# Layer 0's first modulation sums on four TensorE column strips, and a pooling mixer with channels on partitions

## The chip, the core and the metric

The kernel runs on one core of one Trainium2 chip. The metric is device time in microseconds (us) of one execution, as the median of several. Five engines of the core appear below: PE (TensorE, matrix products; PEld is its weight load), DVE (VectorE), ACT (ScalarE), POOL (GpSimd) and SP (SyncE, whose queue issues every DMA of this kernel).

## The reference, cut to what matters

A trunk of two layers over 256 tokens of 2048 channels, all in float32. Layer 0 mixes tokens by pooling, layer 1 by latent attention; each mixer is followed by a SwiGLU feed-forward network (FFN) of 5632 hidden units. What the change concerns is layer 0 up to its FFN:

```python
sc = jax.nn.silu(c)                                   # [1, 2048]
shift_m, scale_m, gate_m, shift_f, scale_f, gate_f = jnp.split(sc @ mod_w[0] + mod_b[0], 6, axis=-1)
h = modulate(rmsnorm(x, norm_mix[0]), shift_m, scale_m)      # h*(1+scale)+shift
# pool_mixer: in each of 4 groups of 512 channels, the mean over the last 2, 4, 8 or 16 tokens less h,
# times a 512x512 matrix of the group, times pool_scale
y = pool_mixer(h, pool_w[0], pool_scale[0])
x = x + gate_m[:, None, :] * y
h = modulate(rmsnorm(x, norm_ffn[0]), shift_f, scale_f)
x = x + gate_f[:, None, :] * swiglu(h, ffn_gate[0], ffn_up[0], ffn_down[0])
```

The six vectors of 2048 are sums over 2048 rows of `mod_w[0]`, 16.8 MB of weights each.

## The kernel before, in words

Tokens are two tiles of 128, channels 16 row tiles of 128 (`KD`) or 4 chunks of 512 (`ND`, `CH`). All weights pass through one pool of six load buffers (`raw`, 1 MB each). Their DMAs are issued in program order by SP, and a load waits until its buffer has been read by the work that used it six loads earlier. PSUM is eight banks (`ps`). Each engine executes its own instructions strictly in a fixed order that a scheduler (or, between `tc.manual_schedule()` lines, the text) set when the program was built.

**The front**, up to the first product of the FFN, does this:

1. Small loads, `x`, the statistics of `x` (`stat_piece`, L410: ACT squares and sums a 128x512 piece; eight pieces; then `rstd`).
2. Shift of the mixer, then scale (`mod_part`, class `Part`): for each of 16 row tiles a 1 MB load, and one DVE instruction (L183) that multiplies the 128x2048 tile by a column of silu(c) and adds it to an accumulator. At the end 16 PE products with ones (L275, `to_cols`) sum over partitions and put the vector on partitions. Between the two sums PE makes the pooled means of `x` (L719 to L728, four groups).
3. The gate (`SharedPart`): 11 row tiles on DVE, five (`GM_PE`) on PE as products with a replicated column (L200), so that the gate stands on all partitions in four banks.
4. Mixer: modulated means (L797, L799), times the group's matrix (L784, 64 instructions with tokens on the output's partitions), copied by ACT (L786), scaled by `pool_scale` on DVE (L791), times the gate, added to `x` and squared again (`add_gated`, L525, L526, L410). This stretch is in an order written out by hand, in which units of the next sums (`pump`) are placed among the steps.
5. Shift and scale of the FFN's first 512 channels (`BlockPart` with `shared`): eight units of two row tiles of 2x512 columns, 1 MB; half of the tiles on PE (L230, one output row), half on DVE (L233); the ends are summed by 16 small products (L247). The result goes to `cols` (L737, L738).
6. The first chunk of the normed stream is scaled (L432), turned (L444), modulated (L458, L459) and meets the first FFN weights, which ACT and DVE split into two parts (L368, L370): the first product of L392.

After that the FFN and layer 1 run as one long row of PE products (L392), with the remaining modulation sums ("background") loaded and added on DVE beside them; this part of the source is the same in both kernels.

## Time and profile before

| | |
|---|---|
| runs, us | 1964.61, 1965.02, 1966.27 (median 1965.02) |
| profiled execution: span from first to last instruction, us | 1962.3 |
| busy in the span, us | PE 1853.0, PEld 1520.7, DVE 1546.4, ACT 850.0, POOL 35.9 |
| loaded and stored | 572.66 MB, mean 292 GB/s |
| mean granted TensorE clock | 0.983 |

The profile is of one execution. A row of the timeline gives the start in us, the time from there to the end of the last of its instructions, the engine, the source line, the operation with its output and inputs, the count, and in brackets how long the engine had stood idle and what ended that. In a table of stretches each engine has its busy time and (x) its instructions, then come the granted PE clock (PEclk), the share of time in which the DMA engines were busy, and the rate. SPq rows are issues of DMAs, not their duration. A row that lists minimum, median and maximum gives the duration of single instructions in ns. A float32 product is two PE instructions ("passes").

### The profile page before, as it was taken

Reading aid. Unit: us, or ns where it says so; the run is one execution under the profiler, and the core shown is the slowest. Engines: PE = TensorE matmul, PEld = TensorE weight load, DVE = VectorE, ACT = ScalarE, POOL = GpSimd, SP = SyncE. Lnnn points to the kernel's source line nnn. Section 1 sums busy time; section 2 is a strip of 40 time slices with the busy share of each in tenths; the row PEclk is TensorE's granted clock in tenths of the full one; section 3 lists DMA queues with packets and bytes.
Section 4 is the critical chain, followed back from the end, with each engine's and each line's share of the span. In section 5 each row is a group of like instructions: output and inputs, shape, how many; then the busy total and the mean of one; then the engine's idle time right before and its main releaser. Section 6 shows DMA issues by size and latency. Waiting matters only on the chain. (4 is left out here: it accounts for less than half of the span.)

```text
span 1962.3 us, 21516 instructions
## 1 busy us (share of the span) xinstructions
PE 1853.0 (94%) x8485; PEld 1520.7 (77%) x8485; DVE 1546.4 (79%) x1312; ACT 850.0 (43%) x939; POOL 35.9 (2%) x33
## 2 busy tenths in 40 slices
PE   0489999999999999998999999999999999999998
PEld 0444888888888888886789987888888888888886
DVE  7887899998778778888989975889986566554556
ACT  3123544444443333334676744544444433343333
POOL 1000000000000000000000000000000000000000
PEclk9889999999999999999899999999999999999999
DMA  9999998898898989987888684989887667665561
GB/s 377 408 378 365 379 321 305 310 350 327 313 329 302 332 325 345 338 333 284 307 311 304 228 295 142 360 303 325 297 293 260 225 229 257 235 209 186 195 219 70
DMA packets 225184, 572.66 MB, mean 292 GB/s; under 512 B 11958, under 2 KB 16286, under 8 KB 203442
## 3 DMA queue, kind: packets, MB, share of 16 engines
q1 hardware_dynamic: 225084, 571.30, 80.9%
q8 instruction: 66, 1.08, 0.2%
q14 instruction: 34, 0.28, 0.0%
HBM read 564.97 MB, written 6.29 MB: 291 GB/s over the span
## 5 line engine op out<-in xcount | busy, mean ns | idle before, releaser
L392 PE MATMUL ps<-hl,act 128*128 128x512 f32 x7008 | 1609.5, 391 | 4.7 <-ACT act L459 2.2
L392 PEld LDWEIGHTS ps<-hl,act 128*128 128x128 f32 x7008 | 1315.1, 188 | 279.3 <-ACT act L459 4.4
L370 DVE TENSOR_TENSOR hl<-raw,hl 128x2048 fp32r<-128x2048 f32 x296 | 676.2, 2289 | 239.9 <-ACT hl L368 236.1
L368 ACT ACTIVATE hl<-raw 128x2048 fp32r<-128x2048 f32 x296 | 566.4, 1919 | 608.7 <-PE ps L392 542.1
L183 DVE SCALAR_TENSOR_TENSOR acc<-raw,s_col,acc 128x2048 f32<-128x2048 f32 x155 | 364.0, 2348 | 4.2 <-DMA raw<-in_mod_w_dram 1.6
L233 DVE SCALAR_TENSOR_TENSOR acc<-raw,s_col,acc 128x1024 f32<-128x1024 f32 x121 | 155.0, 1281 | 8.7 <-DMA raw<-in_mod_w_dram 7.2
L556 DVE TENSOR_TENSOR act<-ps,act 128x512 f32<-128x512 f32 x96 | 64.6, 687 | 14.1 <-PE ps L392 13.7
L275 PE MATMUL ps<-ones,acc 128*128 128x1 f32 x64 | 13.9, 352 | 62.8 <-DVE acc L183 39.9
L410 ACT ACTIVATE junk<-x 128x512 bf16<-128x512 f32 x40 | 25.2, 630 | 89.6 <-DVE x L526 44.1
L275 PEld LDWEIGHTS ps<-ones,acc 128*128 128x128 f32 x64 | 13.8, 332 | 64.5 <-DVE acc L183 41.4
L590 ACT ACTIVATE act<-ps 128x512 fp32r<-128x512 f32 x44 | 23.8, 596 | 61.5 <-PE ps L587 53.4
L625 DVE TENSOR_TENSOR x<-ps,x 128x512 f32<-128x512 f32 x32 | 22.1, 691 | 35.4 <-PE ps L392 35.4
L458 ACT ACTIVATE t2k<-ps,cols 128x256 f32<-128x256 f32 x64 | 33.2, 567 | 21.6 <-PE ps L444 17.0
L634 ACT ACTIVATE t2k<-ps 128x512 f32<-128x512 f32 x24 | 14.2, 593 | 64.2 <-PE ps L392 64.2
L918 PE MATMUL ps<-act,hl 128*128 128x256 f32 x128 | 37.2, 291 | 0.6 <-DVE hl L370 0.6
L919 PE MATMUL ps<-act,hl 128*128 128x256 f32 x128 | 36.7, 287 | 0.0
L920 PE MATMUL ps<-act,hl 128*128 128x256 f32 x128 | 36.1, 286 | 0.0
L591 DVE TENSOR_TENSOR act<-ps,act 128x512 fp32r<-128x512 f32 x44 | 28.2, 685 | 8.1 <-ACT act L590 8.0
L638 DVE TENSOR_TENSOR t2k<-ps,t2k 128x512 f32<-128x512 f32 x24 | 16.6, 690 | 21.3 <-PE ps L392 21.3
L444 PE MATMUL ps<-con,t2k 128*128 128x128 f32 x144 | 22.5, 306 | 11.2 <-DVE t2k L432 8.1
L784 PE MATMUL ps<-act,act 128*128 128x512 f32 x64 | 30.7, 644 | 0.9 <-issue 0.9
L554 ACT ACTIVATE act<-ps 128x512 f32<-128x512 f32 x32 | 19.1, 598 | 28.3 <-PE ps L392 28.1
(168 smaller groups left out, 955.0 us busy)
## 6 DMA issues: line engine op xcount, KB each, us to landing
raw<-in_mod_w_dram SPq DMA_DIRECT2D x128, 1024.0 KB
raw<-in_ffn_gate_dram SPq DMA_DIRECT2D x88, 1024.0 KB
raw<-in_ffn_up_dram SPq DMA_DIRECT2D x88, 1024.0 KB
raw<-in_ffn_down_dram SPq DMA_DIRECT2D x88, 1024.0 KB
raw<-in_mod_w_dram SPq DMA_DIRECT2D x128, 512.0 KB
raw<-in_kv_mod_w_dram SPq DMA_DIRECT2D x32, 1024.0 KB
raw<-in_w_o_dram SPq DMA_DIRECT2D x16, 1024.0 KB
raw<-in_w_uq_dram SPq DMA_DIRECT2D x8, 768.0 KB
```

The costliest lines, as they stand in the source:

```text
L183: dve.scalar_tensor_tensor(out=self.acc, in0=r, scalar=s_col[:, self.kt:self.kt + 1], in1=self.acc, op0=ALU.mult, op1=ALU.add)
L233: dve.scalar_tensor_tensor(out=self.acc, in0=r[:, k], scalar=s_, in1=self.acc, op0=ALU.mult, op1=ALU.add)
L368: hi_ins = act.activation(hi, r, AF.Copy)
L370: lo_ins = dve.tensor_tensor(out=lo, in0=r, in1=hi.bitcast(F32), op=ALU.subtract)
L392: pe.matmul(banks[tok], lhsT=t_[:, i, k, tok * P:(tok + 1) * P], rhs=w[:, k, :], start=first and n < len(part), stop=last and n >= len(ord ...
L458: act.activation(full, pts[k // 2][:, k % 2, :], AF.Identity, scale=scale, bias=bias)
L556: dve.tensor_tensor(out=part, in0=banks[tok], in1=part, op=ALU.add)
L591: dve.tensor_tensor(out=m[:, 1, :, ts_], in0=v, in1=m[:, 0, :, ts_].bitcast(F32), op=ALU.subtract)
L784: pe.matmul(pt, lhsT=pooled[g // 2][:, g % 2, k, tok * P:(tok + 1) * P], rhs=wp[g][:, k, :], start=k == 0, stop=k == KL - 1)
L918: pe.matmul(pt[:, h, :], lhsT=wl(h0 + h, k), rhs=t_[:, 0, k, :], start=k == 0, stop=False)
L919: pe.matmul(pt[:, h, :], lhsT=wh(h0 + h, k), rhs=t_[:, 0, k, :], start=False, stop=False)
L920: pe.matmul(pt[:, h, :], lhsT=wh(h0 + h, k), rhs=t_[:, 1, k, :], start=False, stop=k == KL - 1)
```

## The change

- **Column strips.** Shift, scale and gate of the mixer and the first block of the FFN's shift and scale are summed on PE alone. A new tile `front` holds silu(c) in column 0 of 32-column blocks, zeros elsewhere; its part `s_strip[:, kt, :]` is the stationary operand (128x32). A 1 MB weight tile is multiplied by four products (`StripPart`), each on 512 of its columns and each writing 32 of the 128 partitions of one PSUM bank; in `StripBlock` the four are two row tiles by shift and scale. After the last tile `strip_columns` copies the bank with ACT and turns it with four products by a selector (`sel`, `pair`: new constants), which gives the vector on partitions. DVE adds the bias, which is loaded and turned once (`brows`, `bcol`).
- **Mixer with channels on partitions.** `x` is turned as it comes (`xT`, eight banks of four transposes). The group products have the channels on the output's partitions (L835, 128x256), and `pool_scale` is folded into the gate column (`gm_col`). DVE adds gate times product to `xT` (L849); PE turns the result back (L855), ACT copies token tile 0 of it and DVE token tile 1 into `x`, and the statistics follow.
- **Order of loads.** The small loads come first, then four tiles of the shift, then `x` and the band matrices. `tc.manual_schedule()` around the mixer is gone.
- `SharedPart`, `GM_PE`, the shared form of `BlockPart`, `psc` and the loads for it are removed.

```diff
+    class StripPart:
+        def unit(self):
+            if self.kt == 0:
+                self.bank = ps_t()
+            r = raw_t([P, D])
+            sync.dma_start(r, self.w[self.kt * P:(self.kt + 1) * P, :])
+            for i in range(NSTRIP):
+                pe.matmul(self.bank[i * STRIP:(i + 1) * STRIP, :], lhsT=s_strip[:, self.kt, :],
+                          rhs=r[:, i * CH:(i + 1) * CH], start=self.kt == 0, stop=self.kt == KD - 1)
+            self.kt += 1
+            if self.kt == KD:
+                self.done(strip_columns(self.bank, sel))
...
+    def strip_columns(bank, picks):
+        rows = t2k([P, CH])
+        act.activation(rows, bank, AF.Copy)
+        n = picks.shape[1]
+        pt = ps_t()
+        for b in range(KL):
+            pe.matmul(pt[:, b * n:(b + 1) * n], lhsT=rows[:, b * P:(b + 1) * P], rhs=picks, start=True, stop=True)
...
-    push(mod_part(0, 0, shift_to(C_SM0, to_cols)))
-    push(mod_part(0, 1, scale_to(C_AM0, V_NM, to_cols)))
-    pump(KD)
+    push(strip_cols(0))
+    push(strip_cols(1, vcol[:, V_NM:V_NM + KD]))
+    pump(4)
+    for tok in range(NT):
+        load_x(tok)
...
+    pump(KD - 4)
...
+    xT = [act_t([P, 2, KL, T], F32) for _ in range(2)]
+    for g in range(ND):
+        for h2, pt in enumerate(turned_pieces([x[:, tok, g * CH:(g + 1) * CH] for tok in range(NT)])):
+            act.activation(xT[g // 2][:, g % 2, 2 * h2:2 * h2 + 2, :], pt, AF.Copy)
...
-    gm = SharedPart(a["mod_w"][0][:, cs], a["mod_b"][0:1, cs], lambda acc: None)
-    push(gm)
-    for j in range(ND):
-        push(sf_block(0, j, C_SF0, C_AF0, j == 0), KD // 2)
+    push(strip_cols(2, ps_col))
+    push(first_block(), KD // 2)
+    for j in range(1, ND):
+        push(sf_block(0, j, C_SF0, C_AF0), KD // 2)
...
+                pe.matmul(pt[:, i, :], lhsT=wp[g][:, k, ns], rhs=pooled_of(g * KL + k), start=k == 0,
+                              stop=k == KL - 1)
...
+            with urgent():
+                dve.scalar_tensor_tensor(out=stream_of(kt), in0=pooled_of(kt), scalar=gm_col[:, kt:kt + 1],
+                                         in1=stream_of(kt), op0=ALU.mult, op1=ALU.add)
+        for tok in range(NT):
+            with urgent():
+                pt = ps_t()
+                for k in range(KL):
+                    pe.transpose(pt[:, k * P:(k + 1) * P], stream_of(g * KL + k)[:, tok * P:(tok + 1) * P], ident)
+                piece = x[:, tok, g * CH:(g + 1) * CH]
+                if tok == 0:
+                    act.activation(piece, pt, AF.Copy)
+                else:
+                    dve.tensor_copy(piece, pt)
+                stat_piece(tok, g)
```

**Where instructions stand, first place: the pooled means.** Before, PE's queue has these rows at the end of the shift (`acc_163`) and at the first group of means (`hl_120` is the band, `t2k` pieces of the normed `x`); the sums themselves are on DVE.

```order
L275 MATMUL ps_214<-ones,acc_163 128x1 x16
L719 MATMUL ps_239<-hl_120,ones 128x256
L720 MATMUL ps_239<-hl_120,ones 128x128
L726 MATMUL ps_243<-hl_120,t2k_235 128x256
L727 MATMUL ps_243<-hl_120,t2k_237 128x128
```

Now PE's queue has, at the same place, the last tile of the shift (`raw_250`), the selection (L216), the turning of `x` (two of eight banks shown), the first and the last rows of the four groups of means, and behind them the first tile of the scale (`raw_398`).

```order
L230 MATMUL ps_105<-raw_250,front 32x512 x4
L216 MATMUL ps_258<-con,t2k_256 128x4 x4
L465 MATMUL ps_269<-con,x 128x128 x4
L465 MATMUL ps_310<-con,x 128x128 x4
L750 MATMUL ps_321<-hl_132,ones 128x256
L757 MATMUL ps_391<-hl_132,t2k_377 128x256
L758 MATMUL ps_391<-hl_132,t2k_379 128x128
L230 MATMUL ps_397<-raw_398,front 32x512 x4
```

What moved: the sums of the scale now stand in the same queue as the pooled means, behind all of them.

On SP the loads around that place now read as follows (`raw_250` is the last load of the shift, `raw_398` to `raw_428` the first six of the scale, `raw_434` the seventh, which takes the buffer of `raw_398`).

```order
L228 DMA raw_250<-in_mod_w_dram 128x2048
L228 DMA raw_398<-in_mod_w_dram 128x2048
L228 DMA raw_428<-in_mod_w_dram 128x2048
L809 DMA act_503<-in_pool_w_dram 128x4x512
L228 DMA raw_434<-in_mod_w_dram 128x2048
```

One load of the group matrices stands ahead of `raw_434`, the other three behind the scale's last load.

**Second place: the end of the front.** Before, PE's queue ends the front with the last of L230, the turning of the first chunk of the normed stream (L444), the end of the first block (L247), and the first product of the FFN.

```order
L230 MATMUL ps_589<-raw_676,s_col 1x512
L444 MATMUL ps_682<-con,t2k_666 128x128
L247 MATMUL ps_695<-ones,t2k_696 128x1 x4
L247 MATMUL ps_695<-ones,acc_585 128x1 x8
L392 MATMUL ps_749<-hl_722,act_726 128x512
```

Now it ends with the block's last unit (L251), one of its four selections, the turning back of the stream (L855, 32 rows, the first and the last shown), the other selections, the turning of the first chunk, and the first product.

```order
L251 MATMUL ps_745<-raw_795,front 32x512 x4
L216 MATMUL ps_804<-con,t2k_802 128x2
L855 MATMUL ps_823<-con,act_267 128x128
L855 MATMUL ps_843<-con,act_267 128x128
L216 MATMUL ps_804<-con,t2k_802 128x2 x3
L855 MATMUL ps_891<-con,act_268 128x128 x4
L465 MATMUL ps_909<-con,t2k_905 128x128
L413 MATMUL ps_941<-hl_814,act_919 128x512
```

And ACT's queue behind the gate has the copy of the block's bank, the split of the first FFN weights, four copies into `x`, eight squares with a second split among them, and the modulation (L479).

```order
L212 ACTIVATE t2k_802<-ps_745 128x512
L389 ACTIVATE hl_814<-raw_812 128x2048
L858 ACTIVATE x<-ps_823 128x512
L858 ACTIVATE x<-ps_843 128x512
L431 ACTIVATE junk_829,ssq_818<-x 128x512
L431 ACTIVATE junk_877,ssq_818<-x 128x512
L389 ACTIVATE hl_979<-raw_977 128x2048
L431 ACTIVATE junk_897,ssq_818<-x 128x512
L479 ACTIVATE t2k_920<-ps_909,cols 128x256
```

What moved: the stream's turning back, its copies and its statistics stand behind the block's last unit; before, the stream's statistics (L410 after L526) stood beside the block's sums on other engines, and only L444 to L459 were behind them.

More of the change, by code (lines that the diff above doesn't have):

```diff
@@ L47 @@
 C_FOLD = C_SIGN + 1
-C_END = C_FOLD + P
+C_SEL = C_FOLD + P
+C_PAIR = C_SEL + 4
+C_END = C_PAIR + 2
 BAND_W = T + P
@@ L184, in add @@
                                      in1=self.acc, op0=ALU.mult, op1=ALU.add)
-    class SharedPart(Part):
-        def add(self, r):
-            if self.kt == 0:
-                self.banks = [ps_t() for _ in range(ND)]
-            if self.kt not in GM_PE:
-                super().add(r)
-                return
-            rep = t2k([P, P])
-            act.activation(rep, ones, AF.Copy, scale=s_col[:, self.kt:self.kt + 1])
-            for j in range(ND):
-                js = slice(j * CH, (j + 1) * CH)
-                if self.kt == KD - 1:
-                    pe.matmul(self.banks[j], lhsT=ones, rhs=self.acc[:, js], start=False, stop=False)
-                pe.matmul(self.banks[j], lhsT=rep, rhs=r[:, js], start=self.kt == GM_PE[0], stop=self.kt == KD - 1)
+    def strip_columns(bank, picks):
[5 more added lines that the diff above has]
+            pe.matmul(pt[:, b * n:(b + 1) * n], lhsT=rows[:, b * P:(b + 1) * P], rhs=picks, start=True, stop=True)
+        return pt[:, :KL * n].rearrange("p (b i) -> p i b", i=n)
@@ new lines, in tile_trunk, with __init__, unit @@
+    class StripBlock:
+        def __init__(self, w, col, done):
+            self.w, self.col, self.done, self.kt = w, col, done, 0
+        def unit(self):
+            if self.kt == 0:
+                self.bank = ps_t()
+            r = raw_t([P, 2, 2, CH])
+            rows = self.w[self.kt * P:(self.kt + 2) * P, :].rearrange("(k p) (i n) -> p k i n", p=P, i=2)
+            for k in range(2):
+                sync.dma_start(r[:, k], rows[:, k, :, self.col:self.col + CH])
+            for k in range(2):
+                for i in range(2):
+                    m = (2 * k + i) * STRIP
+                    pe.matmul(self.bank[m:m + STRIP, :], lhsT=s_strip[:, self.kt + k, :], rhs=r[:, k, i, :],
+                              start=self.kt == 0, stop=self.kt == KD - 2)
+            self.kt += 2
+            if self.kt == KD:
+                self.done(strip_columns(self.bank, pair))
@@ L821, in tile_trunk @@
+    rstd = stat_finish()
+    first = modulated(turned_pieces(scaled(rstd, 0, True)), 0, C_AF0, C_SF0)
     push(mod_part(0, 5, gate_to("ffn0")))
```

180 lines of the change are left out of this document (80 added, 100 removed).

## The prediction

> **What bounds the kernel now.** I read the page first: the slices of the span and the chain that ended last.
>
> ```profile
> PE   0489999999999999998999999999999999999998
> PEclk9889999999999999999899999999999999999999
> DMA  9999998898898989987888684989887667665561
> ...
> PE 38%; ACT 0%; DVE 0%; issue 0%; POOLq 0%; ACTq 0%
> ```
>
> A slice is 49 us. PE is full from the fourth on, and as far back as the chain reaches it is PE. The change touches only what comes before, the first 184 us, where PE is idle or half busy and the DMA engines are full. So I asked for stretches: the start, a quiet piece, the three around a dip, the block's loads, and the FFN.
>
> ```profile
> 0.00:4.00 4.00, 0.00 (x0) 0.00 (x0) 0.00 (x0) 1.59 (x2) 3.47 (x8) 1.00 0.51 164
> 20.00:40.00 20.00, 0.00 (x0) 0.00 (x0) 18.87 (x9) 3.59 (x7) 0.00 (x0) 1.00 1.02 422
> 143.00:146.00 3.00, 3.00 (x9) 1.33 (x8) 3.00 (x3) 0.00 (x0) 0.00 (x0) 1.00 0.06 25
> 146.00:149.00 3.00, 3.00 (x9) 1.33 (x8) 0.42 (x1) 0.00 (x0) 0.00 (x0) 1.00 0.91 311
> 149.00:152.00 3.00, 3.00 (x9) 1.32 (x8) 0.00 (x0) 0.00 (x0) 0.00 (x0) 1.00 0.77 242
> 172.00:180.00 8.00, 5.66 (x31) 3.09 (x29) 6.98 (x9) 3.52 (x5) 0.70 (x1) 1.00 1.05 389
> 184.32:600.00 415.68, 415.53 (x1864) 343.93 (x1865) 364.68 (x289) 191.63 (x171) 6.39 (x4) 1.00 0.92 331
> ```
>
> The DMA share (last but one) is 1.0 in the front, so the front is a row of loads with one hole. From 184.32 on PE rests 0.15 us in 416. Hence one number decides: when the FFN's first product starts. Whatever moves it moves the end by as much. The timeline around it shows what it waits for.
>
> ```profile
> 148.72 18.14 SPq L219 DMA_DIRECT2D raw<-in_mod_w_dram  x16
> 167.70 0.37 SPq L381 DMA_DIRECT2D raw<-in_ffn_gate_dram  x1
> 172.24 0.19 ACT L410 ACTIVATION_READ_ACCUMULATOR junk<-x 128x1 f32 x1
> 173.90 0.88 DVE L432 TENSOR_SCALAR t2k<-x,rstd 128x512 f32<-128x512 f32 x2 [0.82 <-POOL rstd L415]
> 174.47 1.36 PE L444 MATMUL ps<-con,t2k 128*128 128x128 f32 x8
> 174.70 5.24 DVE L233 SCALAR_TENSOR_TENSOR acc<-raw,s_col,acc 128x1024 f32<-128x1024 f32 x4
> 177.05 1.91 ACT L368 ACTIVATE hl<-raw 128x2048 fp32r<-128x2048 f32 x1 [1.89 <-DMA raw<-in_ffn_gate_dram]
> 180.00 2.90 PE L247 MATMUL ps<-ones,acc 128*128 128x1 f32 x16 [2.30 <-DVE acc L233]
> 183.25 0.56 ACT L458 ACTIVATE t2k<-ps,cols 128x256 f32<-128x256 f32 x1 [4.29 <-DVE cols L738]
> 184.32 3.03 PE L392 MATMUL ps<-hl,act 128*128 128x512 f32 x6 [1.43 <-ACT act L459]
> ```
>
> The first FFN weights landed at 177.05. They are 1.05 MB and stand right behind the block's last load, so that load landed 2.7 us earlier at 389 GB/s, at about 174.3. From there to the first product it is 10.0 us: DVE's last sums, L247, and 1.1 us from L458 to the product. The stream itself was ready early: its statistics ended at 172.43, its first chunk was turned at 175.83.
>
> **The change part by part.** The same weights are loaded in the same order of vectors, so I sum what changes of the time to the first product.
>
> *Sums leave DVE.* Between 143 and 152 the DMA engines stood still for 0.94, 0.09 and 0.23 of 3 us each, 3.8 us in all, while SP waited for the gate's products on PE to free buffers, as its queue's waits say (us in all, times, longest):
>
> ```profile
> SPq L219 <- PE ps L200: 10.7, 4, 5.6
> SPq L176 <- PE ps L200: 7.8, 1, 7.8
> ```
>
> With strips a buffer is free as soon as PE has read it: **-3.8**.
>
> What does a strip unit cost? No row shows products on column strips. The nearest are four products on four 32-row strips (L702), and ordinary ones with a single output column (L230).
>
> ```profile
> L702 PE MATMUL ps<-t2k,ones x8: 1052/1120/1217, 14.2 to 15.7; 1*128 1x512 f32 x8
> 14.22 2.55 PE L702 MATMUL ps<-t2k,ones 1*128 1x512 f32 x8 [6.20 <-DMA t2k<-in_pool_scale_dram]
> 162.36 12.18 PE L230 MATMUL ps<-raw,s_col 128*1 128x512 f32 x28
> ```
>
> L702's eight passes lasted 1.12 us each and were done in 2.55, so 8 x 1.12 / 2.55 = 3.5 were in flight. L230's 28 follow one another at 0.435, eight of them 3.5 us. A strip unit is also four float32 products, eight passes. Its bounds are 0.9 (two rounds of 0.435, all four strips at once) and 3.5 (nothing overlaps). I take half of L702's 2.55, 1.3, because PE ran at half its later speed so early (the next fence shows such a pair). Against 2.49 us per load (1.05 MB at 422 GB/s) a unit is then hidden under the loads. The Trainium skill ("TensorE: Matmul & The Clock Gate", Part 3) gives 2.38 times for three column strips and says that column strips behave like row strips; with 2.38 the unit would be 3.5 / 2.38 = 1.5, an estimate, and the sum the same.
>
> *Pooled means stop the loads.* PE's queue now has all pooled means between the shift's last strip and the scale's first. Meanwhile SP can issue six scale loads (six buffers) and one of the group matrices; the next waits for the scale's first strip. That covers 6 x 2.49 + 2.7 = 17.6 us from the landing of the shift's last load. What PE does in that time is in these rows.
>
> ```profile
> 59.85 3.77 PE L275 MATMUL ps<-ones,acc 128*128 128x1 f32 x17
> 63.48 1.20 PE L719 MATMUL ps<-hl,ones 128*128 128x256 f32 x2
> 69.10 0.60 PE L719 MATMUL ps<-hl,ones 128*128 128x256 f32 x2
> 72.38 0.60 PE L719 MATMUL ps<-hl,ones 128*128 128x256 f32 x2
> 78.71 0.38 PE L727 MATMUL ps<-hl,t2k 128*128 128x128 f32 x2
> 96.78 48.84 SPq L176 DMA_DIRECT2D raw<-in_mod_w_dram  x16
> 246.41 1.03 PE L444 MATMUL ps<-con,t2k 128*128 128x128 f32 x8
> ```
>
> L719 shows the two speeds, 1.20 and 0.60. The steps: last strip 1.3; ACT's copy of the bank 0.7; eight selecting passes like L275's, 3.77 / 17 = 0.22, 1.8; 32 transposes, 0.11 each after the pace of 246.41 (1.03 less the last one's run-out, over eight), 3.5, or 7 at half speed, taken 4.6; the means, 79.09 - 63.48 = 15.6 from a slow start or 4 x (72.38 - 69.10) = 13.1, taken 14.0 because the transposes run just before; the scale's first strip 1.3; and until data flow again 1.7 (0.66 MB had come by 4.0 us, so flow began at 2.4, after x had been issued at 0.7), or 0.7 (issues ended at 145.62, and the share of 0.91 puts the flow at 146.3). Together 25.4, so the DMA engines stand idle for **+7.8**. Lowest: 0.9 + 0.7 + 0.9 + 3.5 + 13.1 + 0.9 + 0.7 = 20.7, idle 3.1. Highest: 2.55 + 0.7 + 1.8 + 7 + 15.6 + 2.55 + 1.7 = 31.9, idle 14.3. Before, the same means cost no load, since DVE freed the buffers.
>
> *Small loads first.* The bytes are the same. At most the 0.66 MB of the first 4 us come later, 1.6 us; at least nothing. Before, small loads stood between the two halves of x, so I take **+0.5**.
>
> *Group products and gate strips share PE.* After the scale, 64 products of 256 columns meet 16 strip units.
>
> ```profile
> 109.89 30.70 PE L784 MATMUL ps<-act,act 128*128 128x512 f32 x64 [0.90 <-issue]
> ```
>
> L784's 64 passes of 512 columns took 30.7 with a slow start; 128 passes of 256 are the same columns. With 16 x 1.3 and the selections' 1.8 that is 53 us of PE against 3 x 2.7 + 16 x 2.49 = 48 us of loads. PE falls 5 us behind, within the six buffers' 15, so I take **0**; at most 3. The Trainium skill ("TensorEngine Tiling (Array Packing)", Key Properties) says that a change of tiling mode drains the engine, and here strips alternate with full products about a dozen times. No run here shows it; if each of 24 changes exposed 0.16 us, that would be 3.8 us of PE, still within the buffers.
>
> *The tail behind the block.* The stream's last part now stands behind the block's last strip on PE, and then in a row on ACT.
>
> ```profile
> 6.40 0.63 ACT L410 ACTIVATE junk<-x 128x512 bf16<-128x512 f32 x1
> 7.16 0.63 ACT L410 ACTIVATE junk<-x 128x512 bf16<-128x512 f32 x1
> 69.77 0.58 ACT L728 ACTIVATE act<-ps 128x512 f32<-128x512 f32 x1
> ```
>
> From the landing of the block's last load: strip 1.3, ACT's copy 0.6, two selecting passes 0.45, 23 transposes until the first bank that ACT copies is complete (0.16 each between 0.11 and 0.21, 3.7), run-out 0.3: 6.4. Then ACT: four copies at 0.6, eight squares at 0.76 (7.16 - 6.40), one split of weights 1.9 (L368) among them: 10.4. Then from the last square to the first product as before: 172.43 to 173.90, on to 175.83, and 1.1, together 4.5. That is 21.3 instead of 10.0: **+11.3** (8.9 to 13.3 with the bounds of strip and transposes). DVE's update of the stream (16 instructions) needs the gate alone and lies beside the block's loads, 8 x 2.7 = 22 us; were that cover gone, it would still not be on this path, since PE reaches the transposes only behind the block.
>
> *Sum*: -3.8 + 7.8 + 0.5 + 0 + 11.3 = +15.8. The profiled span of 1962.3 becomes 1978.1. Its time stands 2.7 below the median of 1965.02, so the median becomes **1980.8**. With the bounds: -3.8 + 3.1 + 0 + 0 + 8.9 = +8.2 (1973) to -3.8 + 14.3 + 1.6 + 3 + 13.3 = +28.4 (1993).
>
> **The rivals.**
>
> *The loads flow better (not slower).* Place: SP's queue between 54 and 144 us. If the slower pace there came from DVE's late release of buffers, strips would restore 422 GB/s.
>
> ```profile
> 60.00:140.00 80.00, 56.16 (x193) 37.49 (x193) 68.33 (x48) 17.32 (x36) 2.76 (x2) 0.79 1.01 406
> ```
>
> At that rate (last column) these 80 us hold 77.0 us of loads at 422, so 3 us would be won. If also the means on PE fit into the 17.6 us of cover, the hole is gone: -3.8 + 0 + 0.5 - 3 + 8.9 = +2.6, 1967.6, no change that can be told; with a tail shorter than I have it, faster. It decides at a PE phase of 17.6 us; the row that speaks against it is the means' own 13.1 to 15.6, with 4 us left for everything else. Chance 0.17.
>
> *Strips overlap in pairs only.* If the second pass of a strip holds back the next strip, a unit is five rounds of 0.435, 2.2 us. Loads still hide single units, but the gate's stretch becomes 30.7 + 1.8 + 16 x 2.2 = 68 us of PE against 48, 20 behind; the block's eight units, at 2.2 against 2.7, regain 4, so PE reaches the tail some 16 late, and strips in the other terms cost 0.9 more thrice: 15.8 + 16 + 2.7 = +34.5, 1999. L702's 3.5 in flight speak against it, L702 using rows and not columns for it. Chance 0.08.
>
> *Strips do not overlap at all.* 56 units of 3.5 are 196 us of PE; with means 14, transposes 4.6, group products 30.7, selections 5.4, the first load's 9 and the tail's 20 the first product comes at 280, +95: 2060. Chance 0.06.
>
> **How the numbers follow.** My forecast has 0.69. Less than 0.2% (3.9 us) is what a measurement of this kernel can hardly tell from no change; all of the forecast's range lies above it. Of the first rival's 0.17, 0.11 fall within 0.2% and 0.06 below. So slower 0.83, same 0.11, faster 0.06. The range reaches down to the first rival, 1967, and up to the forecast's own 1993; left out are the faster ends and the two strip rivals, 0.2 together. The forecast alone has 1973 to 1993.
>
> **What would show it.** The first FFN product (L413) at about 200 us instead of 184.32, and PE full behind it. A hole in the DMA share of some 8 us around 72 to 80 us, with SP waiting for PE there. Strip units of about 1.3 us. Between the block's last strip and the first product 20 us, half of them ACT's copies and squares. I am wrong if the first product comes before 186, if the loads never pause, or if the transposes (L855) run between the block's units; and if PE shows units of 2.2 or 3.5 us, one of the strip rivals holds.

## The result, and the profile after

| | before | after |
|---|---|---|
| median of runs, us | 1965.43 (1964.61 to 1966.27, 4 runs) | 1984.67 (1981.67 to 1986.31, 4 runs) |
| span of the profiled execution, us | 1962.3 | 1983.5 (of a run of 1985.3) |
| PE busy in the span, us | 1853.0 | 1897.0 |
| first FFN product starts at, us | 184.32 | 203.98 |

The changed kernel is slower: ratio 1.0095, 95% interval 1.0081 to 1.011. PE's slices and the chain, after:

```profile
PE   4887999999999999999899999999999999999998
...
PE 37%; ACT 0%; DVE 0%; issue 0%; POOLq 0%; ACTq 0%
```

PE is full from the fifth slice on (from the fourth before: the fourth, 149 to 198 us, is now a 7) and alone in the chain, so the front decides as before. Stretches of the changed kernel (columns as before: PE, PEld, DVE, ACT, POOL, then PEclk, DMA share, GB/s), and for the start the same two numbers of both kernels up to about where the shift's last load lands (56.5 after, 54.4 before):

```profile
20.00:40.00 20.00, 8.52 (x40) 0.96 (x40) 7.05 (x22) 6.24 (x18) 0.85 (x1) 0.96 0.98 396
66.00:76.00 10.00, 10.00 (x64) 9.23 (x63) 0.00 (x0) 8.35 (x16) 0.00 (x0) 1.00 0.64 251
76.00:86.00 10.00, 9.32 (x77) 4.51 (x75) 0.00 (x0) 2.18 (x4) 0.00 (x0) 1.00 0.46 163
120.00:130.00 10.00, 10.00 (x52) 6.87 (x51) 0.89 (x3) 1.20 (x2) 0.00 (x0) 0.99 1.01 420
140.00:150.00 10.00, 10.00 (x56) 5.87 (x55) 0.00 (x0) 1.20 (x2) 0.00 (x0) 1.00 0.91 321
150.00:163.00 13.00, 12.76 (x88) 5.61 (x86) 0.00 (x0) 1.31 (x3) 0.00 (x0) 1.00 0.92 306
203.98:620.00 416.02, 416.02 (x1864) 345.06 (x1865) 363.51 (x288) 188.88 (x169) 6.39 (x4) 0.99 0.90 323
```

```profile
0.00:56.50 56.50, 26.28 (x122) 3.20 (x122) 7.96 (x30) 9.67 (x22) 3.11 (x10) 0.91 0.93 372
```

```profile
0.00:54.40 54.40, 2.95 (x9) 1.18 (x9) 42.63 (x39) 16.02 (x33) 5.09 (x10) 1.00 0.94 381
```

There are two places where the DMA engines rest. Between 66 and 86 us the share is 0.64 and 0.46, so 3.6 + 5.4 = 9.0 us are lost. Between 140 and 163 the share hardly falls but the rate does, from 420 to 321 and 306 GB/s: 10 x (420 - 321) / 420 + 13 x (420 - 306) / 420 = 5.9 us. From 203.98 on PE never rests. The timeline of the first hole, and what SP waited for:

```profile
56.54 1.07 PE L230 MATMUL ps<-raw,front 128*32 128x512 f32 x8 [0.78 <-DMA raw<-in_mod_w_dram]
...
59.64 6.61 PE L465 MATMUL ps<-con,x 128*128 128x128 f32 x32
...
79.28 5.36 PE L230 MATMUL ps<-raw,front 128*32 128x512 f32 x48
80.41 14.71 SPq L228 DMA_DIRECT2D raw<-in_mod_w_dram  x10
85.31 1.06 PE L230 MATMUL ps<-raw,front 128*32 128x512 f32 x8 [0.68 <-DMA raw<-in_mod_w_dram]
```

```profile
SPq L228 <- PE ps L230: 82.3, 32, 21.4
```

After the shift PE makes the selection (behind a gap of 0.7 us for ACT's copy), the turning of x and the means, and has no other pause until 79.28. Six scale loads lie ready by then; they are done in one row of 48 passes. SP's next load is issued at 80.41, after its longest wait of 21.4 us, and PE gets it at 85.31, 4.9 us later.

In the second place PE's row, behind the scale's last strip (109.34), is group products (L835) and gate strips (L230) in turn, and at its end the last six strips together:

```profile
109.34 1.94 PE L230 MATMUL ps<-raw,front 128*32 128x512 f32 x8 [0.64 <-DMA raw<-in_mod_w_dram]
...
115.10 9.69 PE L835 MATMUL ps<-act,act 128*128 128x256 f32 x32 [1.18 <-DVE act L827]
...
125.71 2.86 PE L835 MATMUL ps<-act,act 128*128 128x256 f32 x12
...
131.85 1.06 PE L230 MATMUL ps<-raw,front 128*32 128x512 f32 x8
132.84 2.43 PE L835 MATMUL ps<-act,act 128*128 128x256 f32 x10
135.20 1.06 PE L230 MATMUL ps<-raw,front 128*32 128x512 f32 x8
...
157.37 5.39 PE L230 MATMUL ps<-raw,front 128*32 128x512 f32 x48
```

A strip comes every 3.35 us (131.85 to 135.20) and frees one buffer, where a load needs 2.49. The tail:

```profile
185.10 1.05 PE L251 MATMUL ps<-raw,front 128*32 128x512 f32 x4 [0.30 <-DMA raw<-in_mod_w_dram]
...
187.16 3.25 PE L855 MATMUL ps<-con,act 128*128 128x128 f32 x28
189.90 2.07 ACT L858 ACTIVATE x<-ps 128x512 f32<-128x512 f32 x4 [0.20 <-PE ps L855]
...
201.35 2.06 PE L465 MATMUL ps<-con,t2k 128*128 128x128 f32 x8 [9.88 <-DVE t2k L453]
203.98 0.79 PE L413 MATMUL ps<-hl,act 128*128 128x512 f32 x1 [0.56 <-ACT act L480]
```

The block's last load is there at 185.1, the first product follows 18.9 us later (10.0 before). PE waits 9.88 us of that for ACT's squares and what hangs on them.

### The profile page after: what moved, and what is told of

It is laid out like the page before. It is cut to its first block, busy times and chain, and to the rows that moved or that the text cites. A ratio compares the mean times of both kernels' runs of the same rounds, so it can differ in the third digit from the quotient of the medians.

```text
span 1983.5 us, 22274 instructions
## 1 busy us (share of the span) xinstructions
PE 1897.0 (96%) x8914; PEld 1530.0 (77%) x8914; DVE 1429.7 (72%) x1267; ACT 853.3 (43%) x944; POOL 30.2 (2%) x30
## 5 line engine op out<-in xcount | busy, mean ns | idle before, releaser
L389 ACT ACTIVATE hl<-raw 128x2048 fp32r<-128x2048 f32 x296 | 566.3, 1917 | 613.7 <-PE ps L413 527.9
L206 DVE SCALAR_TENSOR_TENSOR acc<-raw,s_col,acc 128x2048 f32<-128x2048 f32 x112 | 262.7, 2346 | 0.9 <-DMA raw<-in_mod_w_dram 0.8
L273 DVE SCALAR_TENSOR_TENSOR acc<-raw,s_col,acc 128x1024 f32<-128x1024 f32 x112 | 143.4, 1280 | 3.6 <-DMA raw<-in_mod_w_dram 2.1
L230 PE MATMUL ps<-raw,front 128*32 128x512 f32 x384 | 64.5, 771 | 34.8 <-DMA raw<-in_mod_w_dram 34.8
L230 PEld LDWEIGHTS ps<-raw,front 128*32 128x32 f32 x384 | 9.3, 120 | 81.5 <-DMA raw<-in_mod_w_dram 68.5
L479 ACT ACTIVATE t2k<-ps,cols 128x256 f32<-128x256 f32 x64 | 33.1, 566 | 20.4 <-PE ps L465 20.1
L465 PEld LDWEIGHTS ps<-con,t2k 128*128 128x128 f32 x144 | 19.3, 159 | 24.7 <-issue 13.3
L835 PEld LDWEIGHTS ps<-act,act 128*128 128x128 f32 x128 | 25.2, 204 | 13.1 <-issue 9.6
```

The source lines that it names most:

```text
L206: dve.scalar_tensor_tensor(out=self.acc, in0=r, scalar=s_col[:, self.kt:self.kt + 1], in1=self.acc, op0=ALU.mult, op1=ALU.add)
L230: pe.matmul(self.bank[i * STRIP:(i + 1) * STRIP, :], lhsT=s_strip[:, self.kt, :], rhs=r[:, i * CH:(i + 1) * CH], start=self.kt == 0, stop= ...
L273: dve.scalar_tensor_tensor(out=self.acc, in0=r[:, k], scalar=s_col[:, self.kt + k:self.kt + k + 1], in1=self.acc, op0=ALU.mult, op1=ALU.add)
L389: hi_ins = act.activation(hi, r, AF.Copy)
L465: pe.transpose(pt[:, kk, tok * P:(tok + 1) * P], pieces[tok][:, (2 * h2 + kk) * P:(2 * h2 + kk + 1) * P], ident)
L479: act.activation(full, pts[k // 2][:, k % 2, :], AF.Identity, scale=scale, bias=bias)
```

## The experiments

The theory: the change put two waits into the fixed order of PE's queue, one where strips (which free load buffers) stand behind other work, one where the stream stands behind strips. The rivals differ from run to run and stand in the expectations. Each kernel was timed in turn with the kernel before on the same chip; ratios are to that one. Small differences between two variants are not told apart by their times: the changed kernel's own runs spread over 4.6 us, and the intervals of e5, e7, e8, e9 and e9t overlap its own (1.0081 to 1.011). There the positions in the trace count, and each of them is of one execution.

**Strips of the scale between the groups of means (e1).**

```diff
             act.activation(pooled[g // 2][:, g % 2, 2 * h2:2 * h2 + 2, :], pt, AF.Copy)
-    pump(KD)
+        pump(KD // ND)
```

> The changed kernel (1984.7 us), but with four strip units of the scale placed on PE behind each of the four groups of pooled means, instead of all sixteen behind the last group. Nothing else moves. Theory (PE's queue order holds the buffers): the scale's first strip now stands behind the first group only, at about 66.1 + 3.3 = 69.4 us, before the six buffers' cover ends at 56.5 + 17.6 = 74; the hole of 8.9 us at 70 to 82 us goes, and the first product of the FFN moves by as much: 1976 us, 1974 to 1978. Rival (the hole is not what the loads wait for, or what it costs is regained by the gate's stretch, where PE is busy without a break from 112 to 163 us): the hole goes but PE arrives at the gate no earlier than about 3 us sooner, 1982 us or more.

Measured: 1973.5 us, ratio 1.0039 (1.0025 to 1.0053), 11.2 below the changed kernel. Stretches of this kernel, then the block's last strip and the first product of the FFN:

```profile
66.00:76.00 10.00, 10.00 (x74) 5.82 (x73) 0.00 (x0) 6.03 (x12) 0.00 (x0) 1.00 0.94 364
140.00:150.00 10.00, 10.00 (x68) 4.84 (x70) 0.00 (x0) 1.19 (x2) 0.00 (x0) 1.00 0.99 389
```

```profile
172.47 1.05 PE L251 MATMUL ps<-raw,front 128*32 128x512 f32 x4 [0.30 <-DMA raw<-in_mod_w_dram]
...
191.34 12.88 PE L413 MATMUL ps<-hl,act 128*128 128x512 f32 x46 [0.56 <-ACT act L480]
```

The hole is all but gone (the share of 0.94 leaves 0.6 us of it), and with the order of PE alone. The gain is 12.6 us at the first product (203.98 to 191.34), more than the 9.0 of the hole: the rate between 140 and 150 rose from 321 to 389 too, and in this execution the turning of x took 5.26 us instead of 6.61. The theory holds, its size was too small; the rival is out.

**The stream ahead of the block's strips (e2).**

```diff
-    pump(KD // 2)
-    w_early(ffn_weights(0)[GATE][0:CH, 0:CH])
     stat_start()
...
+    with tc.issue_after(back.ins):   # back: the last turning of the stream
+        pump(KD // 2)
+    w_early(ffn_weights(0)[GATE][0:CH, 0:CH])
     rstd = stat_finish()
```

> The changed kernel, but with the stream's update, its turning back and its statistics ahead of the block's eight strips on PE and ahead of the block's selections on ACT. Theory (the tail is an order, not work): the gate is there at 163.5 us, the stream is turned and squared by about 180 us beside the block's loads, which still end at 185 us; behind them stay one strip (1.1), the bank's copy (0.7), the selections (0.5), the first chunk's turn and modulation (3.0) and the first split, if that stands behind it on ACT (1.9): 7 us in place of 18.9, so the time falls by 10 to 13 us, 1972 to 1975. Rival (PE and ACT are the bound of this stretch wherever the stream stands, or the block's strips, eight units late, hold its loads back): the last load of the block lands some 6 us later than 185, and at most 6 us are won: 1979 or more.

Measured: 1973.15 us, ratio 1.0044 (1.0031 to 1.0056), 11.5 below. The block's last strip there, the split and the first product:

```profile
184.67 1.05 PE L251 MATMUL ps<-raw,front 128*32 128x512 f32 x4 [0.55 <-DMA raw<-in_mod_w_dram]
...
191.15 1.91 ACT L389 ACTIVATE hl<-raw 128x2048 fp32r<-128x2048 f32 x1
193.12 15.16 PE L413 MATMUL ps<-hl,act 128*128 128x512 f32 x58 [4.71 <-ACT hl L389]
```

The last load comes no later than in the changed kernel, and the tail is 8.5 us instead of 18.9. What is late next is the split of the weights (L389), 4.71 us of waiting. The theory holds.

**Group matrices ahead of the scale (e6).**

```diff
     xT = [act_t([P, 2, KL, T], F32) for _ in range(2)]
+    wp = []
+    for g in range(ND):
+        wp.append(act_t([P, KL, CH], F32))
+        sync.dma_start(wp[g], a["pool_w"][0, g].rearrange("(k p) n -> p k n", p=P))
```

> The changed kernel, with the four loads of the group matrices (1 MB each, buffers of their own) issued ahead of the scale's first load instead of one before the scale's seventh load and three behind its last. PE's queue stays as it is. Theory (what is lost in the hole is DMA time, so any load that needs no strip fills it): three further loads of 2.5 us cover 7.5 of the 8.9 us, the block's last load lands 6 to 8 us before 185, and the time is 1977 to 1979. Rival (the gate's stretch is bound by PE, whose row of group products and gate strips has no break from 112 to 163 us): the scale still ends at about 110 less 0 to 2 us, and the time falls by less than 3 us, 1982 or more.

Measured: 1976.73 us, ratio 1.0057 (1.0045 to 1.007), 7.9 below. The stretches of the hole and one of the gate, then the block's last strip:

```profile
66.00:76.00 10.00, 10.00 (x63) 9.21 (x63) 0.00 (x0) 6.02 (x13) 0.00 (x0) 1.00 1.01 417
76.00:86.00 10.00, 9.39 (x76) 4.38 (x74) 0.00 (x0) 2.12 (x4) 0.00 (x0) 1.00 0.93 363
120.00:130.00 10.00, 10.00 (x61) 5.87 (x60) 0.57 (x2) 1.19 (x2) 0.00 (x0) 1.00 0.60 227
```

```profile
177.86 1.05 PE L251 MATMUL ps<-raw,front 128*32 128x512 f32 x4 [0.30 <-DMA raw<-in_mod_w_dram]
```

PE does the same in the same order; only other bytes fill the hole. The block's last load comes 7.2 us earlier. So what the hole costs is DMA time, and work that waits for no buffer buys it back. It is not free: the group loads no longer stand between the scale and the gate, and there a new hole of 4 us appears (share 0.60 between 120 and 130, where the changed kernel has 1.01), while PE works on the group products.

**Both edits (e3).** The edits of the first two experiments in one kernel.

> Both edits of e1 and e2 in one kernel: four strip units of the scale behind each group of means, and the stream ahead of the block's strips. Theory (two separate waits, one ahead of the gate and one behind it): the gains add; first product of the FFN at 203.98 - 12.64 - 10.86 = 180.5 us, time 1984.7 less 11.2 less 11.5 = 1962, 1960 to 1964. Rival (they share a part, since in e2 the first product came to wait for the split of its weights and not for the stream): less than 18 us are won, 1967 or more.

Measured: 1966.63 us (1962.93 to 1972.04, 11 runs), ratio 1.0005 (0.9996 to 1.0014): the time of the kernel before. 18.0 of the 22.7 us came, so neither theory nor rival had the number. The end of the front, and the loads there:

```profile
166.57 5.36 PE L251 MATMUL ps<-raw,front 128*32 128x512 f32 x48
...
176.88 1.05 PE L251 MATMUL ps<-raw,front 128*32 128x512 f32 x4 [0.60 <-DMA raw<-in_mod_w_dram]
...
185.56 19.66 PE L413 MATMUL ps<-hl,act 128*128 128x512 f32 x76 [4.40 <-ACT hl L389]
```

```profile
164.00:170.00 6.00, 6.00 (x46) 3.47 (x48) 2.48 (x4) 4.22 (x10) 0.00 (x0) 0.81 0.53 171
```

The wait for the split is as long as in e2 (4.40), so that is not what the two share. But the loads stop between 164 and 170 (share 0.53): the block's strips now stand behind the stream, PE reaches them only at 166.57, and by then all six buffers are full. The last load came 4.4 us later than in e1 (176.88 against 172.47). Some 3 us of that are this pause, the same kind of wait as the first hole, made by my own edit. Another 1.2 us stand in the first hole, where PE's order is that of e1: the share between 66 and 76 us is 0.82 here and 0.94 there.

**Some of the strips ahead, and the split first (e4).** The edit places four of the block's eight units ahead of the stream and four behind it. In the schedule that was built two came to stand among the first turnings of the stream on PE and six behind them; on ACT the split came ahead of the modulation.

```diff
+    pump(KD // 4)
     stat_start()
...
     with tc.issue_after(back.ins):
-        pump(KD // 2)
+        pump(KD // 4)
...
-    first = modulated(turned_pieces(scaled(rstd, 0, True)), 0, C_AF0, C_SF0)
+    turned = turned_pieces(scaled(rstd, 0, True))
+    with tc.issue_after(last_split[0].ins):   # the ACT part of the split
+        first = modulated(turned, 0, C_AF0, C_SF0)
```

> e3 with two more moves. Some of the block's strips stand ahead of the stream's turning again, so that their buffers come free while PE waits for DVE's update of the stream; and on ACT the split of the first FFN weights stands ahead of the first chunk's modulation, not behind it. Theory (in e2 the first product waited 4.7 us for the split, which stood 3.0 us behind the modulation though its weights had landed at 187.4; and the block's loads paused about 2 us): the first product comes 3 to 4 us before that of e3, at 177 us, time 1958, 1957 to 1960. Rival (a split ahead of the modulation holds ACT until the weights are there, and the modulation then comes as late as the split did): no more than 1 us below e3.

Measured: 1960.01 us (1957.77 to 1961.35), ratio 0.9968 (0.9956 to 0.9981): faster than both kernels. The end of the front:

```profile
172.21 1.05 PE L251 MATMUL ps<-raw,front 128*32 128x512 f32 x4 [0.30 <-DMA raw<-in_mod_w_dram]
174.89 1.91 ACT L389 ACTIVATE hl<-raw 128x2048 fp32r<-128x2048 f32 x1 [0.98 <-DMA raw<-in_ffn_gate_dram]
...
178.07 27.16 PE L414 MATMUL ps<-hl,act 128*128 128x512 f32 x112 [2.12 <-ACT act L481]
```

The last load is back at 172.2, the tail is 5.9 us, and the first product comes 25.9 us earlier than in the changed kernel. This trace is of the fastest of the five runs (1957.77); by the medians the gain is 24.7 us. The split waits for its own load now and for nothing else; the rival is out.

**Half of the group products (e10).** For the second DMA loss: only the inner loop of the group products is cut.

```diff
-                for k in range(KL):
+                for k in range(KL // 2):
```

> The changed kernel, but each group product sums over two of its four row tiles only, which leaves out half of the mixer's products (64 passes of 0.21 us, 13.7 us of PE) and nothing else. Theory (PE's unbroken row from 112 to 163 us sets the pace of the gate's loads; their last six landed 18.9 us apart in all instead of 15.0): the gate's loads keep 2.5 us, the first product of the FFN comes 3.9 us earlier, 1980.8, 1980 to 1982. Rival (the slower loads there have another cause, or DVE's update of the stream and the block's loads hide it): no change, 1984.7 within 0.7.

Measured: 1977.57 us, ratio 1.0067 (1.0055 to 1.008), 7.1 below the changed kernel. A stretch of the gate, then the first product:

```profile
140.00:150.00 10.00, 5.32 (x36) 0.72 (x32) 0.00 (x0) 0.00 (x0) 0.00 (x0) 0.80 1.02 422
```

```profile
197.56 6.73 PE L413 MATMUL ps<-hl,act 128*128 128x512 f32 x22 [0.56 <-ACT act L480]
```

The rate is back at 422 GB/s, with the first hole as it was. The first product comes 6.4 us earlier. PE's row sets the pace of the loads there. I had counted the gate's last six loads alone (3.9 us) and missed what the block's first loads lose.

**x ahead of the shift's tiles (e5); half of x as the very first load (e7).**

```diff
-    pump(4)
     for tok in range(NT):
         load_x(tok)
...
     rope_tables()
+    pump(4)
```

> The changed kernel, with x, the band matrices and the position tables ahead of the first four tiles of the shift, as they stood before. Theory (the 2.1 us by which the shift's last load lands later come from the order of small and large loads): it lands at 54.5 instead of 56.5, and the time falls by 1 to 2 us, 1983 to 1984. Rival (those 2 us come from the other small loads that now stand ahead, the bias rows and constants): no change, 1984.7 within 0.5.

```diff
+    load_x(0)
     sync.dma_start(con, a["con"])
...
-    for tok in range(NT):
-        load_x(tok)
+    load_x(1)
```

> The changed kernel, with one change at its very start: the first half of x (1 MB) is issued as the first load, ahead of the small ones, as before the change. Theory (e5 has shown that x ahead of the shift's tiles doesn't bring the shift earlier, 57.2 us; what is lost is the stretch in which SP issues nine small loads, 0.7 to 4.7 us, with no large load under way): the shift's last load lands at 54.9 instead of 56.5, and the time falls by 1.6 us, 1982.5 to 1983.6, if PE's pace in the means stays. Rival (the issue of small loads costs nothing, the bytes are only spread differently): it lands at 56 or later, no change within 0.5 us.

Measured: 1981.84 (ratio 1.0085, 1.0071 to 1.0098) and 1982.67 us (1.0079, 1.0066 to 1.0093). Both medians are 2 to 3 us below the changed kernel, with ranges that overlap its own (1981.02 to 1984.18 and 1977.23 to 1983.24), and neither trace shows the reason given. The shift's last strip, which starts as its load lands (56.54 in the changed kernel), of e5 with two more rows, and of e7:

```profile
57.25 1.87 PE L230 MATMUL ps<-raw,front 128*32 128x512 f32 x8 [0.56 <-DMA raw<-in_mod_w_dram]
...
60.76 3.69 PE L465 MATMUL ps<-con,x 128*128 128x128 f32 x32
...
77.48 5.36 PE L230 MATMUL ps<-raw,front 128*32 128x512 f32 x48
```

```profile
56.34 1.94 PE L231 MATMUL ps<-raw,front 128*32 128x512 f32 x8 [0.56 <-DMA raw<-in_mod_w_dram]
```

56.5 was expected to become 54.5 and 54.9; it became 57.2 and 56.3. Both theories fall: where x stands doesn't set when the shift is loaded. In e5 the turning of x took 3.69 us instead of 6.61, and the scale's strips came 1.8 us earlier (77.48 against 79.28) although the shift came later; that is most of its 2.8 us. In e7 I found no single place for the 2.0, which may be no gain at all.

**The shift's strips twice (e8); group matrices behind the scale, without (e9) and with that (e9t).** The first kernel repeats every shift strip into a bank that nothing reads; the second moves the one group load that stood ahead of the scale's seventh load behind its last one; the third does both.

```diff
+            if self.twice:
+                again = ps_t()
+                for i in range(NSTRIP):
+                    pe.matmul(again[i * STRIP:(i + 1) * STRIP, :], lhsT=s_strip[:, self.kt, :],
+                              rhs=r[:, i * CH:(i + 1) * CH], start=True, stop=True)
```

```diff
-        sync.dma_start(wp[g], a["pool_w"][0, g].rearrange("(k p) n -> p k n", p=P))
+        with tc.issue_after(scale.loads[9].ins):
+            sync.dma_start(wp[g], a["pool_w"][0, g].rearrange("(k p) n -> p k n", p=P))
```

> The changed kernel, in which every strip unit of the shift (the first vector only) is done twice on PE, once into a bank that nothing reads. It adds 16 units of about 1 us to PE and takes none away. Theory (in e5 the 32 transposes of x took 3.69 instead of 6.61 us, since PE had run denser strips before them and was granted a full clock; the half clock in the means' stage is a cost of the change's thin PE load): the clock is up when the shift ends, the transposes take 3.5 to 3.8, the hole of 8.9 shrinks to about 6, and the time FALLS by 1.5 to 3 us although PE does more, 1981.5 to 1983. Rival (the pace of the transposes came from elsewhere, and added strips are just added work): transposes stay at 6 to 7, the last unit's second half adds 1 us, 1984.7 to 1986.

> The changed kernel, with all four loads of the group matrices behind the scale's last load; in the changed kernel one of them stood ahead of the seventh load of the scale and filled 2.5 us of the hole. (In e8 a second one had come to stand there, which mixes two causes; this kernel is the base for e9t.) Theory (each load that needs no strip fills 2.5 us of the hole): the hole grows from 8.9 to 11.4 us, the time to 1987.2, 1986.5 to 1988. Rival (loads ahead of the hole win nothing by themselves, the stretch of the gate being bound by PE): 1984.7 within 0.5.

> e9 with the shift's strips done twice, as in e8, and the order of the loads exactly that of e9: what differs between e9 and this is PE's added work alone. Theory (a denser PE in the shift brings the full clock to the selections and the transposes of x, 6.6 to 3.7 us, and the hole is shorter by that): 2 to 2.5 us below e9, 1985. Rival (e8 won by the second load ahead of the hole alone): within 0.7 us of e9, or above it.

Measured: 1981.69 (ratio 1.0079, 1.0066 to 1.0093), 1980.75 (1.0087, 1.0074 to 1.0101) and 1980.26 us (1.0078, 1.0066 to 1.0091). The turning of x and the scale's first strips in e9, and a stretch of it:

```profile
60.07 3.69 PE L465 MATMUL ps<-con,x 128*128 128x128 f32 x32
76.79 5.36 PE L230 MATMUL ps<-raw,front 128*32 128x512 f32 x48
```

```profile
140.00:150.00 10.00, 10.00 (x56) 6.14 (x48) 0.00 (x0) 1.19 (x2) 0.00 (x0) 1.00 1.01 421
```

In e8 the turning of x took 3.69 us and the time came out as expected, but the kernel mixes two causes, since in it a second group load had moved ahead of the hole. The pair was to part them and could not: e9, without a single added strip, had the fast turning of x in its profiled execution as well. That the sixteen added units cost nothing is all that the pair shows. The time of e9's theory (1987) fell, it came out at 1980.75. Its hole did much as the theory says: the scale's strips began 2.5 us earlier (76.79), by the fast turning, and still the DMA engines lost some 9.2 us there instead of 9.0, since one load less filled it. What was won came later: the rate between 140 and 150 was 421 GB/s instead of 321. With four group loads between scale and gate instead of three, the gate's loads come later and PE lags less behind them. The other kernels are in keeping with that: between 120 and 150 us the mean rate is 326, 334, 382 and 419 GB/s with none (e6), two (e8), three (changed) and four (e9) group loads there. How the time of e9 divides between the turning and these loads can't be told by what was run.

**e4 with x first (e11).** The edits of e4 and e7 together.

> e4 with the first half of x issued as the very first load, as in e7. Theory (what e7 won, 2.0 us, came from bytes under way earlier): 1958, 1957 to 1959. Rival (e7 brought the shift's last load only 0.2 us earlier, 56.3 instead of 56.5; what it won came later, from PE's pace in a stretch that in e4 lies under the loads): 1960 within 0.7.

Measured: 1961.32 us (1959.74 to 1962.65, 11 runs), ratio 0.9982 (0.9973 to 0.9991). No gain on e4, so the theory falls, and the rival's number is missed by 0.6 us too; e4 stays the best version. The two intervals overlap, and the traces differ ahead of the gate in what no edit asked for: the turning of x took 5.19 us here and 3.69 in e4's, and the share between 66 and 76 us is 0.76 against 1.01.

## Why the forecast came out as it did

The direction and both places were right, and so, roughly, was their size; the time is 3.9 us above the forecast. The first product moved by 19.7 us where the sum had 15.8. That the two differences are equal is chance: another 1.5 us were lost behind the first product, and the profiled span stands 1.2 us below the median instead of the 2.7 that I had carried over from before. It is luck, too, that the sum missed by no more: 8.0 us were missing in three terms, and 4.2 came back in two others. Term by term:

| term, us | forecast | measured | from |
|---|---|---|---|
| DMA hole of before goes | -3.8 | -3.8 | it is gone; the gate's new loss is counted below |
| loads otherwise faster than before | (rival) | -1.8 | not measured: what the other rows leave of 19.7 |
| pooled means stop the loads | +7.8 | +9.0 | share 66 to 86; e1, e6 |
| start | +0.5 | +1.4 | 54.4 x 381 = 20.7 MB are reached at 56.5 - (56.5 x 372 - 54.4 x 381) / 420 = 55.8 |
| group products and gate strips share PE | 0 | +5.9 | rates 140 to 163; e10 gives 6.4 |
| tail behind the block | +11.3 | +8.9 | 18.9 against 10.0; e2 |

**Sums leave DVE**: as forecast. The strip unit was taken at 1.3 us; one alone took 1.06 at full clock (85.31), and six done in one row took 5.36 us, 0.89 each, so all four strips overlap and both rivals on that are out. The Trainium skill ("TensorE: Matmul & The Clock Gate", Part 3) has 2.38 times for three strips; here four of them, in two passes each, took 0.89 where eight passes in a row would take 3.5, which is 3.9 times.

**Pooled means**: the mechanism was right, SP's wait and the place (66 to 86) too. Shown by e1 (the order of PE) and e6 (the bytes). The size was 1.2 short, and not because of PE. From the landing of the shift's last load until data flow again it is some 24.8 us (a share of 0.87 between 80 and 90 us puts the flow at 81.3), where the sum had 25.4; that they agree is luck, since the turning of x took 2.0 us more than the 4.6 of the sum and the means 0.8 less than 14.0. But the loads run dry at 72.4 (a share of 0.24 between 70 and 80), 15.9 us after that landing and not 17.6: the cover was too long.

**Group products and gate strips share PE** is the step that failed. I wrote that PE falls 5 us behind, "within the six buffers' 15, so I take 0; at most 3". The 5 us were about right: PE did its last gate strips at 157 to 163, and three group loads and 16 gate loads at 2.49 us each behind the scale's last (109.34) make 156.7. (That was luck in part: the row of products and strips took 47.7 us and not 51.5, and began later than I had it.) But six buffers don't cover 15 us. A load that is issued into an empty queue needs time to come, 4.9 us at 80.41, so the cover is about 10 (an estimate, 6 x 2.49 - 4.9), and the lag must be held against it strip by strip: the buffers come back at PE's pace of 3.35 us for ten loads running. And I took PE's row to begin when the scale ended; it began at 115.1, 5.8 us after the scale's last load. At 2.49 us a load the first gate tile would land at 119.3 and the fifth at 129.3; PE did them at 124.71 and 138.55, so its lag grew from 5.4 to 9.3 us, and just there, at 140, the rate falls. What the runs show in place of the 0 is 5.9 us by the rates, and 6.4 by e10, in which half of the products are left out.

Part of the 3.35 us is the alternation itself. Ten passes of 256 columns take 2.15 (two more passes make 2.43 into 2.86), a strip unit in a row 0.86 (in e1 a row of 40 strip passes took 4.50 us where 48 take 5.36), 3.01 together; so 0.34 us a pair, an estimate of 0.17 for each change between strips and full products, about 3.4 us in ten pairs. The Trainium skill ("TensorEngine Tiling (Array Packing)", Key Properties) says that a change of mode drains the engine; the 0.17 us are in keeping with it. I had priced it at 0.16 and called it covered by the buffers. No run takes it away by itself.

**The tail**: the mechanism was right, 2.4 us too dear. The turning ran at 0.12 a product and not 0.16 (3.25 for 28; the granted clock was 1.00 from 180 to 190 us), so that ACT's first copy starts 4.8 us behind the block's last strip and not 6.4; the rest is ACT's row, whose four copies took 2.07 instead of 2.4. e2 shows that the 8.9 us are an order and no work: with the stream first, DVE's update, the turning and the squares lie under the block's loads.

**Small loads first**: 1.4 instead of 0.5, but the small loads at the very start are hardly it. By 20 us both kernels have loaded 6.2 MB; 0.56 MB, 1.3 us, are lost between 22 and 26 us, where the rates are 285 and 304 GB/s (418 and 430 before). The bytes loaded until then put the loads of the band and the positions there, which are issued behind x. In e5, which issues x, the band and the positions earlier, the rate dips at 13 to 15 us instead, to 165 and 79. So the place of x only moves the dip; why it costs more than before stays open.

**The rivals.** "The loads flow better" was half right: the 1.8 us that are left over speak for it, and so do rows away from both holes (from 86 to 100 us 424 GB/s against 402 before, from 163 to 172 us 386 against 370), but its condition, means that fit under 17.6 us of cover, did not, since PE's phase took until 80.4. Behind the first product another 1.5 us were lost that I had not foreseen (span 1983.5 - 203.98 against 1962.3 - 184.32): PE enters the FFN after 9.88 us of rest and is granted half its clock for longer, as the same stretch behind the first product shows, of before and of after.

```profile
186.40:188.40 2.00, 1.85 (x7) 0.99 (x7) 1.05 (x3) 2.00 (x5) 0.00 (x0) 0.70 1.04 385
```

```profile
206.00:208.00 2.00, 2.00 (x7) 1.51 (x6) 2.00 (x2) 2.00 (x2) 0.00 (x0) 0.50 0.00 0
```

Over the first 6 us behind the first product the mean granted clock is 0.73 before and 0.58 after, which makes some 0.9 of the 1.5 us; what the rest is stays open.

## What to carry to other kernels

When sums move from one engine to another, the freeing of load buffers moves into that engine's queue: go through it in order and ask at each long stretch without such a consumer how many loads are covered, and take off the time that a fresh load needs to come. If consumers alternate with other work, hold the cover against the lag at each of them and not at the end. Here the change itself was sound: with the same work in another order on PE and ACT it went from 1.0% slower to 0.3% faster than before.

## What the runs showed of the hardware that I had not expected

The 32 turnings of x took 6.61, 5.26, 5.00 and 3.69 us in the changed kernel, e1, e2 and e9, which do the same up to there. A stretch within them, of the changed kernel and of e9:

```profile
60.00:62.00 2.00, 2.00 (x11) 2.00 (x10) 0.00 (x0) 0.97 (x2) 0.00 (x0) 0.50 1.06 438
```

```profile
60.00:62.00 2.00, 2.00 (x20) 2.00 (x21) 0.17 (x1) 1.58 (x4) 0.00 (x0) 1.00 1.01 418
```

The granted clock is 0.50 in one and 1.00 in the other. In this front PE is busy less than half of the time with strips (8.52 of 20 us between 20 and 40), and the clock goes up and down; with every shift strip done twice (e8) it was 1.00 from 50 to 70 us. The Trainium skill ("TensorE: Matmul & The Clock Gate", Part 1) has two steps of the clock, set by how busy a free-running window was, and calls the number of slow products variable from run to run; the rows agree with the two steps. It may be why the changed kernel's runs spread over 4.6 us and those of before over 1.7. That is argued and not shown: only the profiled executions show where the clock went down, and the mean clocks of the four runs (0.979, 0.974, 0.978 and 0.973, from the fastest to the slowest) follow their times only in part. It also bears on every position above that hangs on the turning of x, the changed kernel's first hole included: its 6.61 us are the longest of all the kernels.
